# A two-layer hybrid decoder trunk on one core: z gates and output weights moved into the recurrence of layer 1

## The chip, the cores and the metric

The kernel runs on one core of one Trainium2 chip. The metric is the device time of one execution in microseconds (us). Engines are named as in the profile: PE (TensorE matmuls), PEld (its weight loads), DVE (VectorE), ACT (ScalarE), POOL (GpSimd), SP (SyncE, which issues the DMAs). Every engine works through its own instructions in order.

## What is computed

The reference is a trunk of two residual layers over 2048 tokens of width 1024, in float32, with a top-2 mixture of experts behind each mixer. Layer 0 mixes by causal pooling and a convolution. Layer 1, the place of the change, is a gated DeltaNet with 8 heads of width 128:

```python
u = h @ w_in
qkv = silu(causal_depthwise_conv(u[..., :3 * DN_WIDTH], conv_w))
q, k, v = split(qkv)
z = u[..., 3 * DN_WIDTH:4 * DN_WIDTH]
...
v_new = u_i - einsum('bhck,bhkv->bhcv', w_i, state)
o_i = einsum('bhck,bhkv->bhcv', qg_i, state) + einsum('bhcm,bhmv->bhcv', a_i, v_new)
state = state * d_i[..., None, None] + einsum('bhck,bhcv->bhkv', kd_i, v_new)
...
o = o * rsqrt(mean(o * o, -1) + EPS) * onorm_g * silu(z)
y = o @ w_out
x = x + g_m * y
```

The gate silu(z) is not needed before the output projection; q, k and v are needed by the recurrence over chunks, which needs, for each chunk, the inverse of a lower triangular matrix.

## The kernel before

`layer0` and `moe(0)` take the first 1243 us. Layer 1 follows: `mixer1` (`dn_project`, then `dn_chain`), `out_phase(1)`, `moe(1)` and `final`. A tile scheduler orders each engine's instructions when the kernel is built, by priorities that follow the order of the code, and adds the waits; after that the order is fixed.

`dn_project` works on two halves of 1024 tokens, and in each on 8 heads (`dn_head`). A head has four *strips*: 128 output columns of k, q, v and z, in the order k, q, v, z. A strip's 1024x128 weights are loaded by one DMA, split on ACT (`wh`) and DVE (`wl`) into a high and a low part (L237, L238), and multiplied in `proj` as 3 products for each of 8 blocks of the contraction and 2 token halves: 48 matmuls (L260 to L262). k, q and v go through `ub` to a four-tap convolution on DVE (`dacc`, L1218 and L1220) and a Silu on ACT; z gets only a Silu (L1210) and is stored to `zT`. Then PE transposes k and q by blocks (`tk<-ident,kq`, L1230), ACT and DVE take sums of squares (`ssk`, `ssq`), DVE makes `kd`, PE multiplies k by k and q (`tp<-kqh`, L1287), DVE applies the decay (`na`, L1288) and makes `kg` (L1293) and `vp` (L1305). `na`, `kd`, `kg` and `vp` are stored to `stg`. Head by head the scheduler weaves strips of one head into the rest of the other. `egb`, which `kg` reads, has the buffer of `ub`, and `vp` that of `dacc`.

`dn_invert` inverts the diagonal blocks of four heads at a time in 31 steps j of a multiplication and a reduction on DVE (L1321, L1322), whose width grows as j times j. There are four inversions. `pump` lets a head advance one by a number of steps: eight a head. The inversion of half 0's heads 0 to 3 runs in half 0, that of its heads 4 to 7 in heads 0 to 3 of half 1, that of half 1's heads 0 to 3 in the last heads, and the fourth in the recurrence.

`dn_chain` runs 16 blocks of 128 tokens (blocks 0 to 7 read half 0, 8 to 15 half 1). For each block and each group `hg` of four heads, `M` builds the inverse `tt` from the diagonal blocks two blocks ahead, and `R` makes `dv` (L1463: `stin` less a product with the state S), `vt` (by `tt`), the output `po` and the new state S (L1481). `tail` and `O` normalize and transpose the output, and `store` writes it to `yT`. The loads `stin` are issued two blocks ahead into six buffers, in two pools.

`out_phase(1)` begins when the recurrence is over: it loads the eight blocks of `w_out` (L509), splits them (`woh`, `wol`), makes rows of the gate `gm` and the gain on all partitions (`row_bcast`, L199), loads y and z for the first tiles (`yr`, `zr`), multiplies them (L490), and runs `project` for 16 tiles of 128 tokens (`po<-woh,yh`, L536), each followed by the multiplication by `gm` (L540), the residual sum and the norm.

Of the kernel before, what the change touches and what calls it, by code (L numbers as in the profile page):

```python
# [6 lines left out]
F32 = mybir.dt.float32  # L7
# [9 lines left out]
P = 128  # L17
S = 2048
# [23 lines left out]
NYS = 3  # L42

# [27 lines left out]
class Trunk:  # L71
# [120 lines left out]
    def row_bcast(self, psum, src, out):  # L192

        nc = self.nc
        for h in range(2):
            p = psum.tile([P, 512], F32, name="tp")
# [68 lines left out]
    def layer0(self, yT):  # L265
        tc, nc, ins = self.tc, self.nc, self.ins
        with ExitStack() as ctx:
            cv = ctx.enter_context(tc.tile_pool(name="cv0", bufs=1))
            psl = ctx.enter_context(tc.tile_pool(name="psl0", bufs=1, space=PSUM))
# [194 lines left out]
    def out_phase(self, l, yT, xsrc, gm=None, raw=None, cv=None):  # L464
# [4 lines left out]
        with ExitStack() as ctx:  # L469
            ep = lambda name, bufs, **k: ctx.enter_context(tc.tile_pool(name=name, bufs=bufs, **k))  # L470
            wa = ep("woa", 1)
            ys = [ep("yo0", 1), None]
            wb = ep("wob", 1)
            wp = ep("wo", 1)
# [24 lines left out]
            wh = wa.tile([P, KD, D], F32R, name="woh")  # L499
            wl = [p.tile([P, KD // 2, D], F32R, name="wol") for p in (wa, wb)]  # L500
            if raw:
                stage = [raw.tile([P, D], F32, name="wr") for _ in range(KD)]
            else:
# [4 lines left out]
            for k in range(KD):  # L508
                nc.sync.dma_start(stage[k], ins[f"w_out{l}"][k])  # L509
            yin = [load_y(t) for t in range(2)]  # L510
            yin[0] = split_y(0, yin[0])
            for k in range(KD):
                self.prep = self.split(wh[:, k], wl[k // 4][:, k % 4], stage[k])
            if gm is None:
                gm = wp.tile([P, D], F32, name="gm")
                self.row_bcast(pt, self.mod[:, l * 48 + 16:l * 48 + 24], gm)
            ga = wp.tile([P, D], F32, name="ga")
            self.row_bcast(pt, self.gain[l, 1], ga)
            sh = wp.tile([P, D], F32, name="sh")
            self.row_bcast(pt, self.mod[:, l * 48 + 24:l * 48 + 32], sh)  # L520
            wr = wp.tile([P, KD, 36], F32, name="wr")
            nc.sync.dma_start(wr, ins["w_r"][l])
# [5 lines left out]
            def project(t):  # L528
# [11 lines left out]
                nc.vector.tensor_mul(h, ps, gm)  # L540
# [181 lines left out]
    def route_setup(self, pool):  # L722
# [16 lines left out]
        for l in range(2):  # L739
# [8 lines left out]
            self.lists.append(lst)  # L748


    def moe(self, l, raw=None):

# [425 lines left out]
    def pump(self, n):  # L1178
# [3 lines left out]
        with self.tc.issue_after(self.loaded.ins):  # L1182
            next(self.rest, None)
# [513 lines left out]
```

## Time and profile before

| | us |
|---|---|
| median of 3 runs | 3320.69 (3320.61 to 3329.27) |
| the profiled execution | 3314.58 |
| its span, first to last instruction | 3312.9 |
| busy in the span: PE / DVE / ACT / POOL | 2905.9 / 2440.1 / 1495.6 / 1023.9 |
| mean granted clock of PE | 0.943 of full speed |

The profile shows one execution. "Busy" is time in which an engine ran an instruction; the clock is the mean over the stretch of what PE was granted, and 1.00 stands for 2.4 GHz, 0.50 for 1.2 GHz. A row of windows gives the stretch and its length in us, the busy us of each engine with its instructions in brackets, then the clock of PE, the mean busy share of the 16 DMA engines, and GB/s. A timeline row gives when an instruction began; rows of like instructions are drawn together with their count (x14). In brackets stands how long the engine had been idle and which instruction ended that. A matmul's time includes its passage through the array, so neighbouring matmuls overlap: the spacing of their starts is what they cost.

### The profile page before, as it was taken

The page shows a single profiled execution, that of the slowest core. Times are in us where ns is not written, and L with a number is a line of the kernel's source. Part 1 is how long each engine was busy: PE and PEld are TensorE (multiplying, and loading weights), DVE is VectorE, ACT ScalarE, POOL GpSimd, SP SyncE. Part 2 cuts the span into 40 slices and gives each one's busy share as a digit, 9 for nine tenths or more (in the row PEclk, how much of TensorE's full clock was granted, in tenths as well). Part 3 has the DMA queues.
Part 4 walks back from the last instruction along what each step waited for, and adds up shares of the span by engine and source line. Part 5 has one row for each costly group of instructions (what it writes and reads, how often), then busy time and mean ns, then how long its engine had stood idle before and what let it go on. Part 6 is the DMA issues. An engine that isn't in the chain of part 4 may idle for free. (4 is left out here: it accounts for less than half of the span.)

```text
span 3312.9 us, 41950 instructions
## 1 busy us (share of the span) xinstructions
PE 2905.9 (88%) x14192; PEld 2311.3 (70%) x14192; DVE 2440.1 (74%) x3805; ACT 1495.6 (45%) x2560; POOL 1023.9 (31%) x877
## 2 busy tenths in 40 slices
PE   4979878787999997999989999987988996999991
PEld 3756656566777774888867877767986765777770
DVE  4998999757878775767876776858445556888783
ACT  6135233216656546443444433344762224666552
POOL 1142323333444431313212131235530213444431
PEclk9989989888999997999999999998999997999995
DMA  6226233638999854545452343457857437989876
GB/s 222 88 70 213 80 132 127 216 121 302 314 277 302 269 166 156 174 149 192 141 169 87 104 142 114 138 155 220 268 189 223 158 121 251 312 279 298 262 230 217
DMA packets 384987, 633.40 MB, mean 191 GB/s; under 512 B 111232, under 2 KB 245504, under 8 KB 384768
## 3 DMA queue, kind: packets, MB, share of 16 engines
q1 hardware_dynamic: 355904, 563.38, 50.0%
q0 software_dynamic: 28864, 67.30, 8.7%
q8 instruction: 114, 1.87, 0.2%
q14 instruction: 105, 0.86, 0.1%
HBM read 484.46 MB, written 175.44 MB: 199 GB/s over the span
## 5 line engine op out<-in xcount | busy, mean ns | idle before, releaser
L260 PE MATMUL pm<-hh,wh 128*128 128x512 f32 x1408 | 564.9, 402 | 0.8 <-ACT wh L237 0.7
L262 PE MATMUL pm<-hh,wl 128*128 128x512 f32 x1408 | 555.2, 395 | 3.6 <-DVE wl L238 3.6
L261 PE MATMUL pm<-hl,wh 128*128 128x512 f32 x1408 | 554.0, 394 | 4.5 <-DVE hl L233 4.5
L238 DVE TENSOR_TENSOR wl<-wr,wh 128x1024 fp32r<-128x1024 f32 x384 | 452.0, 1217 | 41.6 <-ACT wh L237 38.4
L237 ACT ACTIVATE wh<-wr 128x1024 fp32r<-128x1024 f32 x384 | 399.4, 1057 | 126.4 <-PE pu L819 57.2
L838 POOL DMA_INDIRECT acc<-ys,ixs x102 | 262.8, 2577 | 434.7 <-DVE wl L238 122.0
L261 PEld LDWEIGHTS pm<-hl,wh 128*128 128x128 f32 x1408 | 268.2, 190 | 63.9 <-DVE hl L233 4.9
L260 PEld LDWEIGHTS pm<-hh,wh 128*128 128x128 f32 x1408 | 268.3, 191 | 62.3 <-issue 4.5
L262 PEld LDWEIGHTS pm<-hh,wl 128*128 128x128 f32 x1408 | 267.7, 190 | 62.5 <-DVE wl L238 5.7
L817 PE MATMUL pu<-wh,xt 128*128 128x512 f32 x656 | 268.3, 409 | 0.5 <-ACT xt L237 0.5
L818 PE MATMUL pu<-wl,xt 128*128 128x512 f32 x656 | 260.9, 398 | 0.0
L819 PE MATMUL pu<-wh,xt 128*128 128x512 f32 x656 | 259.8, 396 | 0.0
L238 DVE TENSOR_TENSOR wl<-wraw,wh 128x1024 fp32r<-128x1024 f32 x88 | 110.9, 1260 | 152.1 <-ACT wh L237 152.0
L286 DVE SCALAR_TENSOR_TENSOR acc<-cin,wfir,acc 128x512 f32<-128x512 f32 (+1 forms) x320 | 214.7, 726 | 0.1
L536 PE MATMUL po<-woh,yh 128*128 128x512 f32 x512 | 172.7, 414 | 30.6 <-issue 10.7
L237 ACT ACTIVATE wh<-wraw 128x1024 fp32r<-128x1024 f32 x88 | 93.2, 1059 | 224.5 <-PE pm L261 224.3
L1220 DVE SCALAR_TENSOR_TENSOR dacc<-ub,cols,dacc 128x1024 f32<-128x1024 f32 x144 | 186.7, 1297 | 2.8
L536 PE MATMUL po<-wol,yh 128*128 128x512 f32 x512 | 166.7, 406 | 0.0
L536 PE MATMUL po<-woh,yl 128*128 128x512 f32 x512 | 165.6, 403 | 0.2 <-DVE yl L238 0.2
L795 POOL DMA_INDIRECT xg<-hn,ixs x102 | 112.8, 1106 | 162.5 <-PE tp L805 77.0
L189 POOL TENSOR_TENSOR rs<-rs1t,expo 128x1 f32<-128x1 f32 x48 | 28.3, 589 | 381.3 <-DVE rs1t L187 341.1
L819 PEld LDWEIGHTS pu<-wh,xt 128*128 128x128 f32 x656 | 123.8, 189 | 30.8 <-DVE xt L238 0.5
(377 smaller groups left out, 6359.9 us busy)
## 6 DMA issues: line engine op xcount, KB each, us to landing
wr<-in_w_up_dram SPq DMA_DIRECT2D x256, 512.0 KB, 7.8
wr<-in_w_down_dram SPq DMA_DIRECT2D x128, 512.0 KB, 7.2
modw<-in_modwT_dram SPq DMA_DIRECT2D x96, 512.0 KB, 5.2
wraw<-in_w_in_dram SPq DMA_DIRECT2D x88, 512.0 KB, 3.6
stin<-stg SPq DMA_DIRECT2D x32, 1280.0 KB, 10.5
yr<-yT SPq DMA_DIRECT2D x32, 512.0 KB, 4.2
acc<-xo SPq DMA_DIRECT2D x32, 512.0 KB, 4.1
hn<-ho SPq DMA_DIRECT2D x32, 512.0 KB, 3.1
```

The source lines that it names most:

```text
L237: a = nc.scalar.activation(h, x, AF.Copy) if eng == "act" else nc.vector.tensor_copy(h, x)
L238: return a, nc.vector.tensor_sub(l, x, h.bitcast(F32))
L260: nc.tensor.matmul(ps, wh[:, k], hh[:, k], start=k == 0, stop=False)
L261: nc.tensor.matmul(ps, wh[:, k], hl[:, k], start=False, stop=False)
L262: nc.tensor.matmul(ps, wl[:, k], hh[:, k], start=False, stop=k == KD - 1)
L286: self.tap = nc.vector.scalar_tensor_tensor(o, x, w, i, op0=ALU.mult, op1=ALU.add)
L536: nc.tensor.matmul(ps[:, ns], a[:, k], b[:, ns], start=k == 0 and i == 0, stop=k == KD - 1 and i == 2)
L817: nc.tensor.matmul(ps, xh[:, k], uh, start=k == 0, stop=False)
L818: nc.tensor.matmul(ps, xh[:, k], ul, start=False, stop=False)
L819: nc.tensor.matmul(ps, xl[:, k], uh, start=False, stop=k == KD - 1)
L838: st = nc.gpsimd.indirect_dma_start(out=self.acc, out_offset=bass.IndirectOffsetOnAxis(ap=ix[:, 0:1], axis=0), in_=ys, in_offset=None, bou ...
L1220: nc.vector.scalar_tensor_tensor(acc, ub[:, i:i + 1024], self.col("dn_conv", si * 4 + i), acc, op0=ALU.mult, op1=ALU.add)
```

## The change

In half 1 the z strips leave `dn_head`. `z_strips`, a generator, holds all eight and is handed to `dn_chain`, which runs one strip at each `run(side)` in its first blocks; the weights, the activations hT and z buffers live in pools on the right side of the memory until then. The heads of half 1 advance an inversion by four steps a head (`pump(2 - half)`) instead of eight, so only the second inversion runs there; the third and the fourth run in `dn_chain`, two steps at each `run(invs, invs)`.

When the strips are through, `right.close()` frees their memory and `weights()` follows: it loads the eight blocks of `w_out`, three buffers in turn, multiplies each by the row of the gate (so `out_phase(1)` no longer does), splits it, and makes the rows `ga`, `sh` and `wr` (`out_rows`). `out_phase(1)` finds them in `self.outw`. In `dn_chain`, `dv` is written over `stin`'s VP, `vt` over KE, the decayed state into the next S; `stin` has four buffers (NST) in one pool, `nd`, `ld` and `ot` have fewer, PSUM gives two tiles to the strips and one to `po`. The z tile is half as wide, with two buffers and two stores a strip. All pools take `reuse_waits="tile"`: a tile waits for the tiles whose place it takes.

```diff
-        with ExitStack() as ctx:
-            ep = lambda name, bufs, **k: ctx.enter_context(tc.tile_pool(name=name, bufs=bufs, **k))
+            ep = lambda name, bufs, **k: ctx.enter_context(tc.tile_pool(name=name, bufs=bufs, reuse_waits="tile", **k))
...
+            rp = lambda name, bufs: right.enter_context(tc.tile_pool(name=name, bufs=bufs, side="right", reuse_waits="tile"))
+            wp = rp("w1", 2)
+            hp = rp("h1", 2)
+            self.zs = rp("z1", 1)
...
+                    if half == 0 and hd % 4 == 3:
                         assert next(self.inv, None) is None
-                        self.inv = self.dn_invert(half, hd // 4, wk) if (half, hd) != (1, 7) else iter(())
+                        self.inv = self.dn_invert(half, hd // 4, wk)
+        def z_strips(psum):
+            for hd in range(8):
+                w = self.load_strip(wp, ins["w_in1"][24 + hd], "d")
+                self.z_strip(1, hd, w, hT, psum)
+                yield
+    def z_strip(self, half, hd, w, hT, psum):
+        nc = self.nc
+        for c2 in range(2):
+            zs = self.zs.tile([P, 512], F32, name="zs", bufs=2)
+            ps = psum.tile([P, 512], F32, name="pm")
+            self.proj(ps, w, hT[c2])
+            nc.scalar.activation(zs, ps, AF.Silu)
+            nc.sync.dma_start(self.zT[half][hd, :, c2 * 512:(c2 + 1) * 512], zs)
...
-        self.pump(2)
+        self.pump(2 - half)
-        strip(3)
+        if half == 0:
+            strip(3)
...
+            def weights():
...
+                for k in range(KD):
+                    w = stage[k]
+                    nc.vector.tensor_mul(w, w, gm)
+                    fetch(k + 2)
+                    yield
+                    self.split(wh[:, k], wl[:, k], w)
+                    yield
+                self.outw = (wh, (wl[:, :4], wl[:, 4:]), *self.out_rows(1, wo, pm, "mm"))
...
+            side = chained(zg, close(), weights())
+            invs = chained(self.dn_invert(1, 0, iv), self.dn_invert(1, 1, iv))
+            for bl in range(NT):
...
+                run(t)
+                run(*r)
+                run(invs, invs)
+                run(*m)
+                if bl + 3 < NT:
+                    load_n(bl + 3)
+                if bl > 1:
+                    store(bl - 2)
+                run(side)
+                run(r[0], m[0])
+                run(invs, invs)
+                run(r[1], m[1])
+                run(invs, invs)
+                run(t)
+                run(r[0], m[0])
+                load(*((bl + 2, 0) if NST > 3 else (bl + 1, 1)))
+                run(side)
+                run(invs, invs)
+                run(r[1], m[1])
...
-                nc.vector.tensor_mul(h, ps, gm)
-                nc.vector.tensor_add(x, h, x)
+                if l == 0:
+                    nc.vector.tensor_mul(h, ps, gm)
+                    nc.vector.tensor_add(x, h, x)
+                else:
+                    nc.vector.tensor_add(x, ps, x)
```

Three places show how the order moves. The first is DVE in the burst of a late half-1 head, before. Here `xtmp` and `xblk` are an inversion's step 25, and the `wl` is that of the next head's k strip:

```order
L1288 TENSOR_TENSOR na<-tp,dt 128x512 x2
L238 TENSOR_TENSOR kql<-kq,kqh 128x512 x2
L1293 TENSOR_TENSOR kg<-kq,egb 128x1024
L1288 TENSOR_TENSOR na<-tp,dt 128x512 x2
L1305 TENSOR_TENSOR vp<-tk,nk 128x1024
L1321 TENSOR_TENSOR xtmp<-xblk 128x25x25
L238 TENSOR_TENSOR wl<-wraw,wh 128x1024
L1322 TENSOR_REDUCE xblk<-xtmp 128x25
```

The same place of the change; the `wl` is now that of the next head's q strip:

```order
L1322 TENSOR_TENSOR kg<-kq,egb 128x1024
L1317 TENSOR_TENSOR na<-tp,dt 128x512
L1322 TENSOR_TENSOR kg<-kq,egb 128x1024
L1334 TENSOR_TENSOR vp<-tk,nk 128x1024
L1350 TENSOR_TENSOR xtmp<-xblk 128x25x25
L1351 TENSOR_REDUCE xblk<-xtmp 128x25
L1350 TENSOR_TENSOR xtmp<-xblk 128x26x26
L239 TENSOR_TENSOR wl<-wraw,wh 128x1024
L1351 TENSOR_REDUCE xblk<-xtmp 128x26
```

The `wl` of the k strip has moved ahead of the burst, where z's was, and that of the q strip stands behind `vp` and one and a half steps. In earlier heads of half 1, with narrower steps, it stands behind three.

The second is DVE in block 1 of the recurrence, from the add of the first group's S to behind that of the second, before:

```order
L1481 TENSOR_TENSOR S_18534<-sd_18436,pr 128x512
L1417 STREAM_TRANSPOSE xt_18449<-xh 128x128
L1417 STREAM_TRANSPOSE xt_18457<-xh 128x128
L1481 TENSOR_TENSOR S_18570<-sd_18445,pr 128x512
L1517 TENSOR_SCALAR ot<-mm,cols 128x512
L1447 COPY w_18118<-mm 128x2x64
L1447 COPY w_18120<-mm 128x2x64
L1517 TENSOR_SCALAR ot<-mm,cols 128x512
```

And the change, in which that `wl` belongs to a z strip and the steps to the third inversion:

```order
L1512 TENSOR_TENSOR S_18055<-S_18055,pr 128x512
L1351 TENSOR_REDUCE xblk<-xtmp 128x28
L1350 TENSOR_TENSOR xtmp<-xblk 128x29x29
L1351 TENSOR_REDUCE xblk<-xtmp 128x29
L1350 TENSOR_TENSOR xtmp<-xblk 128x30x30
L1351 TENSOR_REDUCE xblk<-xtmp 128x30
L1350 TENSOR_TENSOR xtmp<-xblk 128x31x31
L1351 TENSOR_REDUCE xblk<-xtmp 128x31
L239 TENSOR_TENSOR wl<-wraw,wh 128x1024
L1512 TENSOR_TENSOR S_18063<-S_18063,pr 128x512
L1546 TENSOR_SCALAR ot<-mm,cols 128x512
L1481 COPY w_17554<-mm 128x2x64
```

Three and a half inversion steps and a `wl` now stand between the two adds, and the copies of `w` behind them.

The third is PE where the recurrence ends and `out_phase(1)` begins, before:

```order
L1514 MATMUL mm<-ident,on_21191 128x128 x4
L1514 MATMUL mm<-ident,on_21196 128x128 x4
L1514 MATMUL mm<-ident,on_21260 128x128 x4
L1514 MATMUL mm<-ident,on_21265 128x128 x4
L199 MATMUL tp<-ident,mod 128x128 x8
L199 MATMUL tp<-ident,gain_13392 128x128 x8
L199 MATMUL tp<-ident,mod 128x128 x8
L536 MATMUL po<-woh,yh 128x512 x2
L536 MATMUL po<-wol,yh 128x512 x2
L536 MATMUL po<-woh,yl 128x512 x2
```

And the change; `ob` has the part of `on`:

```order
L1543 MATMUL mm<-ident,ob_21111 128x128 x2
L1543 MATMUL mm<-ident,ob_21208 128x128 x4
L1543 MATMUL mm<-ident,ob_21227 128x128 x4
L532 MATMUL po<-woh,yh 128x512 x2
L532 MATMUL po<-wol,yh 128x512 x2
L532 MATMUL po<-woh,yl 128x512 x2
L532 MATMUL po<-woh,yh 128x512 x2
```

The transposes for the rows (L199) are gone from here, and the first product of the output phase follows the last transposes of the recurrence.

## Rows read from the trace of the kernel before

**Rows 1.** Windows: us; busy PE, PEld, DVE, ACT, POOL; clock; DMA share; GB/s.

```profile
1780.00:2190.00 410.00, 387.30 (x1852) 321.68 (x1851) 310.31 (x379) 164.11 (x251) 98.46 (x101) 0.99 0.37 117
...
2206.00:2470.00 264.00, 232.84 (x1848) 221.41 (x1848) 150.75 (x369) 157.77 (x592) 132.80 (x128) 0.95 0.74 231
2470.00:2518.00 48.00, 33.44 (x131) 26.03 (x132) 25.72 (x26) 18.27 (x28) 2.19 (x2) 0.72 0.88 275
```

**Rows 2.** Window from the first to the eighth T0 of half 1.

```profile
1794.64:2176.27 381.63, 358.93 (x1714) 297.80 (x1713) 290.54 (x355) 150.33 (x224) 91.51 (x90) 0.99 0.38 121
```

**Rows 3.** Timeline of PE in half 1: start, duration, line, instruction.

```profile
1794.64 1.91 PE L1230 MATMUL tk<-ident,kq 128*128 128x128 f32 x16
...
2117.22 1.91 PE L1230 MATMUL tk<-ident,kq 128*128 128x128 f32 x16
...
2176.04 0.39 PE L262 MATMUL pm<-hh,wl 128*128 128x512 f32 x1
2176.27 1.36 PE L1230 MATMUL tk<-ident,kq 128*128 128x128 f32 x11
```

**Rows 4.** Groups by line, half-1 heads: busy us, mean ns; idle before, releaser.

```profile
L1321 DVE TENSOR_TENSOR xtmp<-xblk 128x49 f32<-128x49 f32 (+30 forms) x56 | 50.1, 895 | 1.4 <-POOL xblk L1315 0.2
L238 DVE TENSOR_TENSOR wl<-wraw,wh 128x1024 fp32r<-128x1024 f32 x29 | 35.4, 1221 | 66.9 <-ACT wh L237 66.9
...
L1322 DVE TENSOR_REDUCE xblk<-xtmp 128x7 f32<-128x49 f32 (+30 forms) x56 | 30.2, 539 | 1.2
...
L1266 ACT ACTIVATE dt<-dt,brr 128x128 f32<-128x128 f32 x64 | 19.5, 387 | 1.1 <-DVE brr L1262 1.1
```

**Rows 5.** Timeline of DVE, head that begins at 2117.22.

```profile
2119.42 0.75 DVE L1218 TENSOR_SCALAR dacc<-ub,cols 128x1024 f32<-128x1024 f32 x1
...
2124.92 1.28 DVE L1220 SCALAR_TENSOR_TENSOR dacc<-ub,cols,dacc 128x1024 f32<-128x1024 f32 x1
...
2136.89 1.21 DVE L1305 TENSOR_TENSOR vp<-tk,nk 128x1024 f32<-128x1024 f32 x1
...
2139.23 1.22 DVE L238 TENSOR_TENSOR wl<-wraw,wh 128x1024 fp32r<-128x1024 f32 x1
```

**Rows 6.** Timeline of PE: two waits, in brackets idle time and releaser.

```profile
2001.51 0.44 PE L1230 MATMUL tk<-ident,kq 128*128 128x128 f32 x2 [3.34 <-ACT kq L1225]
...
2591.43 1.94 PE L564 MATMUL tp<-ident,ho 128*128 128x128 f32 x8 [4.75 <-DVE ho L547]
```

**Rows 7.** Windows of the 6 us behind those two waits.

```profile
2001.50:2007.50 6.00, 5.94 (x26) 4.78 (x27) 5.21 (x7) 1.15 (x3) 0.30 (x2) 1.00 0.21 78
2591.40:2597.40 6.00, 5.97 (x18) 3.55 (x19) 4.07 (x5) 2.35 (x4) 0.53 (x1) 0.50 0.96 284
```

**Rows 8.** Window from the eighth T0 to block 5 of the recurrence.

```profile
2176.27:2313.42 137.15, 107.54 (x712) 96.23 (x710) 99.45 (x193) 64.70 (x221) 72.35 (x71) 0.88 0.71 218
```

**Rows 9.** Timeline of DVE, last inversion step in the recurrence.

```profile
2306.75 2.48 DVE L1321 TENSOR_TENSOR xtmp<-xblk 128x961 f32<-128x961 f32 x1
...
2309.34 1.15 DVE L1322 TENSOR_REDUCE xblk<-xtmp 128x31 f32<-128x961 f32 x1
```

**Rows 10.** Waits of PE in that stretch: us in total, times, longest.

```profile
PE pr L1379 <- DVE dv L1463: 7.0, 5, 3.4
PE mm L1438 <- DVE tl L1434: 4.6, 8, 0.8
```

**Rows 11.** Window of one later block of the recurrence.

```profile
2374.00:2388.65 14.65, 13.97 (x122) 13.71 (x122) 7.15 (x20) 10.10 (x38) 8.97 (x10) 1.00 0.88 268
```

**Rows 12.** Timeline of PE between recurrence and output phase.

```profile
2472.42 2.53 PE L1514 MATMUL mm<-ident,on 128*128 128x128 f32 x8 [5.12 <-ACT on L1507]
...
2493.10 1.19 PE L536 MATMUL po<-woh,yh 128*128 128x512 f32 x2 [10.67 <-issue]
```

**Rows 13.** Timeline of DVE between those two.

```profile
2484.04 5.77 DVE L238 TENSOR_TENSOR wol<-wr,woh 128x1024 fp32r<-128x1024 f32 x5 [2.01 <-ACT woh L237]
```

**Rows 14.** Groups by line, output phase of layer 1, DVE.

```profile
L540 DVE TENSOR_TENSOR ho<-po,gm 128x1024 f32<-128x1024 f32 x15 | 18.3, 1222 | 45.6 <-PE po L536 45.6
```

More of the change, by code (lines that the diff above doesn't have):

```diff
@@ L42 @@
 NYS = 3
+NST = 4
 def slots():
@@ L497, in split_y @@
                 return yh, yl
[L499 to L503, printed above, removed]
+            if l == 0:
+                wh = wa.tile([P, KD, D], F32R, name="woh")
+                wl = [p.tile([P, KD // 2, D], F32R, name="wol") for p in (wa, wb)]
                 both = wk.tile([P, 2, D], F32, name="wraw", tag="hT", bufs=1)
@@ new lines, in dn_chain, with behind @@
+            both = lambda bl: [load(bl, hg) for hg in range(2)]
+            with tc.high_priority(offset=400):
+                load_n(0)
+                both(0)
+                load_n(1)
+                load(1, 0)
+                if NST > 3:
+                    load(1, 1)
+                last = load_n(2)
+            na, kg, vp = self.stores[-3:]
+            def behind(st, ld):
+                tc.add_manual_dep(st.ins, ld.ins.name,
+                                  mybir.DependencyInfo(mybir.DependencyClass.NoSync, mybir.DependencyReason.DATA),
+                                  reason="issued after the first loads")
@@ new lines, in dn_chain, with chained, close @@
+            behind(na, last)
+            zg = zgen(pz)
+            run(zg)
+            for sd in (kg, vp):
+                behind(sd, last)
+            g = [M(0, 0), M(0, 1)]
+            nxt = [M(1, 0), M(1, 1)]
+            run(*g)
+            for i in range(5):
+                run(*g)
+                if i == 1:
+                    run(*nxt)
+            def chained(*gens):
+                for g in gens:
+                    yield from g
+            def close():
+                right.close()
+                yield
@@ new lines, in dn_chain @@
+            side = chained(zg, close(), weights())
+            invs = chained(self.dn_invert(1, 0, iv), self.dn_invert(1, 1, iv))
+            for bl in range(NT):
+                r = [R(bl, 0), R(bl, 1)]
+                m, nxt = nxt, [M(bl + 2, hg) if bl < NT - 2 else iter(()) for hg in range(2)]
+                t = tail(bl - 1) if bl else iter(())
+                oss[bl] = self.small.tile([P, 2, 4], F32, name="oss")
+                run(t)
[17 more added lines that the diff above has]
+                run(r[1], m[1])
+                load(*((bl + 2, 1) if NST > 3 else (bl + 2, 0)))
+                run(invs, invs)
+                if bl:
+                    O(bl - 1, 0)
+                run(*m)
+                run(invs, invs)
+                if bl:
+                    O(bl - 1, 1)
+                run(*nxt)
+                run(*m)
+                if bl == 4:
+                    for _ in invs:
+                        pass
@@ L1604, in pack @@
+            for _ in side:
+                pass
+            for _ in tail(NT - 1):
+                pass
+            for hg in range(2):
+                O(NT - 1, hg)
+                if hg == 0:
+                    store(NT - 2)
+            store(NT - 1)
 def pack(inputs):
```

266 lines of the change are left out of this document (104 added, 162 removed).

## The prediction

> **What bounds the kernel now.** I read the stages first [rows 1]. They all belong to layer 1, which is where the change moves instructions. In the half-1 heads PE is busy for 387.3 of 410 us at a clock of 0.99: that stage is bound by PE. In the recurrence (2206 to 2470) it is 232.8 of 264, and in the 48 us after it 33.4 at a clock of 0.72. So what can be won without taking work away from PE lies in the recurrence and behind it.
>
> The heads are told by the time between the transposes `tk<-ident,kq` of neighbouring heads; I call that moment T0. From the first T0, 1794.64, to the eighth, 2176.27 [rows 3], there are seven periods in 381.6 us, 54.5 us each, with PE busy for 358.9 [rows 2], 51.3 a head. A strip is 48 matmuls a weight block, two token halves by 24, and they follow each other at 0.23 us [rows 3], so 10.9 us. A head has four.
>
> In such a head DVE works through a burst that starts at T0: the last strip's taps, sums of squares, `kd`, `na`, `kg`, `vp`. In the last full head it ran from 2119.42 to 2138.1, with the `wl` of the next strip at 2139.23 [rows 5]. The z strip is what PE does meanwhile.
>
> **The change: the heads.** Every half-1 head loses its z strip, its `wl` and four of its eight inversion steps. If PE stayed full this would be 7 × 10.9 = 76 us plus the 22.7 that PE idles today (381.6 - 358.9), 99 in all. It cannot stay full: the order of DVE puts the `wl` of the next head's q strip behind `vp` and up to three inversion steps, and PE has only the k strip before it. From that head: `vp` ends 20.9 us after T0 (2117.22 [rows 3]). Without the z strip's `wl` (1.2) and one of two inversion steps in it (2.0) it would end at 17.7; I add 2 for `na`, whose factors ACT scales in 3.1 us (eight of 0.39 [rows 4]). Then come one or two inversion steps (the mean step is 0.90 + 0.54 us [rows 4]), and `wl`, 1.2: that is T0 + 23 to 24, and I let the q strip run freely from T0 + 24. Behind that stand two strips, 21.8, with a few transposes. A period is then 45.9 and seven are 321: **-60 us**. Ends: -99 (PE full), and -22 (every period as long as its PE work of today, idle in the place of z). I take the first sum, as its rows are the nearest.
>
> PE now has some 5.5 us of idle in each head, in pieces of up to 3. Rows on what that does to the clock: after an idle of 3.34 us the next 6 us ran at 1.00; after one of 4.75 the next 6 us ran at 0.50, which is 1.2 in place of 2.4 GHz, and 6 us at half speed lose 3 us [rows 6, 7]. I keep the clock at 1.00, for the pieces are nearer to the first.
> The Trainium skill speaks against this part ("TensorE: Matmul & The Clock Gate", HAM oscillation — how this bites in real kernels): a loop that lets TensorE idle once in every pass falls to the cold clock in every pass and pays the return each time. The trace agrees on single gaps; by that rule 21 us of this term would be lost, and the sum below would be -7.
>
> **The first blocks.** From the eighth T0 to block 5's `tt` product at 2313.42 there are 137.15 us, PE busy for 107.5 at a clock of 0.88 [rows 8]. A clock of 0.88 is 24% of the time, 33 us, at half speed; with PE busy for about 26 of them, 13 us come back at full speed, which leaves 94.5. The seven moved strips add 76: 171 is the floor. Waits stay. Right behind T0 no strip is left: PE needs some 3 us for the transposes (eleven in 1.36 [rows 3]) and twelve `kqh` products, then stands for `vT` and for `na`. The last tap ended 9.0 us after T0 [rows 5], 7.8 without the `wl` ahead of it, and the Silu follows: 9 us of waiting in two pieces. In block 1 the order puts four inversion steps and a `wl` between the two adds on S, and the copy of `w` behind both. The last step measures 2.48 + 1.15 us [rows 9]; the four with the `wl` are about 10 us, and PE has some 4 us of other work there: 6 us. In block 2 a like piece: 4 us. That makes 190, **+53 us**. Ends: 171 (+34), and 171 plus the 29.6 that PE idles there today (+63). I stay between: of today's waits on DVE, 7.0 us on `dv` and 4.6 on `tl` [rows 10], the strips cover the first, but not what stands behind the second inversion.
>
> **Blocks 5 to 15.** A block takes 14.65 us with PE at 13.97, DVE at 7.15, ACT at 10.10 and DMA at 0.88 [rows 11]. A weight adds 2.4 us to DVE (1.22 for gm [rows 14], 1.2 for the split [rows 4]), one copy to ACT, and 0.52 MB, which is 36 GB/s on 268: DVE and ACT have room, DMA comes to 1.0. **+1 us**; the ends are -2 (the two long blocks behind the old inversion shorten) and +10 (every load late by an eighth of a block).
>
> **The start of the output phase.** Today the last transposes run at 2472.42 and the first product at 2493.10, after an idle of 10.67 [rows 12], in which DVE splits the weights, five of them in 5.77 us, and loads follow [rows 13]. Weights, rows and gate are now ready, and the order has the product right behind the transposes. I put it at 2477, for PSUM must be handed over: **-16 us** (ends -10 and -20; if `yr` and `zr` were late, the -10).
>
> **The tiles.** The multiplication by gm, 1.222 us a tile [rows 14], goes. PE covers it except where a group of tiles ends and PE waits for `ho`, as at 2591.43 for 4.75 us [rows 6]: 3 or 4 times, **-4 us** (0 to -8). **Leaner waits** in layer 0 and both MoE stages move no row and free a wait here and there; I take **-2** (0 to -6).
>
> Sum: -60 + 53 + 1 - 16 - 4 - 2 = **-28 us** on the profiled execution, 3314.6 (span 3312.9). The median of the runs, 3320.7, is 0.18% above it, so I forecast **3293 us**. Its own range, from the middle of each term's bounds, is 3273 to 3311.
>
> **Rivals.**
> (1) *PE stays nearly full.* If the order hides the burst behind the k strip and `wl` comes at T0 + 21, a head falls to 43 us, -80 in all, and the strips cover the waits of block 1 and 2, +42: the sum is -59, 3262 us. For it: DVE, busy for 290.5 us in seven heads [rows 2], 41.5 in one, loses four steps and a `wl` and falls to some 35 of 43 us. Against it: its order is fixed and `vp` alone ends at about T0 + 20.
> (2) *The clock falls once a head.* If the pieces of idle run together, 3 us are lost at each of 7 heads and 3 waits of the first blocks: +30, the sum is +2, 3323 us, no change. For it: the row at 4.75 us; against it: the one at 3.34.
> (3) *Slower: the clock falls twice a head,* at the wait for `vT` and at the wait for `wl`. Then 6 us are lost in each of 7 heads, 42, and 12 in the first blocks: +54, the sum is +26, 3347 us. It decides from 4 us lost a head (28 / 7). Against it: the k strip of 10.9 us lies between the two waits.
>
> **How the numbers follow.** Chances: the forecast 0.48, rival 1 0.15, rival 2 0.20, rival 3 0.17. About 0.3%, 10 us, is what a measurement of this kernel can tell from no change. Of the forecast 0.45 is faster and 0.03 the same; rival 1 is all faster; of rival 2 0.03 is faster, 0.14 the same and 0.03 slower; of rival 3 0.01 is the same and 0.16 slower. Faster 0.63, same 0.18, slower 0.19. The range 3260 to 3338 leaves out somewhat under half of rival 1 (0.07) and three quarters of rival 3 (0.13), 0.2 in all.
>
> **What would show it.** T0 to T0 near 46 us, with idle of PE put down to `wl`, and a clock of 1.00 in the heads; if it stands below 0.97, rival 2 or 3. From the eighth T0 to block 5 near 190 us, with waits for `w` in block 1. Blocks of 14.65 us from 5 on. The first `po<-woh` within 5 us of the last transposes of the recurrence. The prediction is wrong if the heads stay above 50 us, or if the first blocks take over 202.

## The result, and the profile after

The changed kernel is **slower**: 3359.14 us median of 4 runs (3356.39 to 3366.02) against 3321.01 (3320.61 to 3329.27) in the same session, a ratio of 1.012 [1.0107, 1.0133]. I had forecast 3293 us, and 3260 to 3338 as the range. The profiled execution has a span of 3358.3 us for 3312.9, +45.4 (the medians differ by 38.1); its mean clock is 0.942 for 0.943.

Cut at the same moments as in the prediction, the two spans compare as follows (us; each end is the start of a PE row, T0 is the `tk<-ident,kq` between two heads, "block n" its first `tt` product):

| stage | before | after | difference | forecast |
|---|---|---|---|---|
| up to the first T0 | 1794.6 | 1795.3 | +0.6 | 0 |
| seven half-1 heads | 381.6 | 359.5 | -22.1 | -60 |
| eighth T0 to block 5 | 137.2 | 211.4 | +74.3 | +53 |
| block 5 to block 15 | 147.4 | 169.1 | +21.7 | +1 |
| block 15 to the first `po<-woh` | 32.3 | 15.3 | -17.0 | -16 |
| output phase, to the first transposes of the MoE | 277.5 | 267.0 | -10.5 | -4 |
| MoE and final norm | 542.3 | 540.7 | -1.6 | -2 (with the first row) |

So the start of the output phase and its tiles came as forecast or better, the last small term came to half of what I had put, and the three large ones all came out worse. The windows of those three, after (columns as in [rows 1]); they answer to [rows 2], [rows 8] and, for a block, [rows 11]:

```profile
1795.28:2154.80 359.52, 299.53 (x1375) 241.76 (x1374) 249.35 (x294) 137.94 (x204) 89.95 (x89) 0.91 0.35 110
2154.80:2366.23 211.43, 180.50 (x1052) 159.95 (x1050) 150.27 (x266) 84.56 (x245) 72.26 (x66) 0.92 0.61 184
2366.23:2535.33 169.10, 149.65 (x1214) 140.73 (x1214) 87.62 (x211) 115.68 (x392) 89.67 (x84) 1.00 0.69 215
2502.78:2519.13 16.35, 14.98 (x122) 13.99 (x122) 8.51 (x23) 10.93 (x39) 9.18 (x9) 1.00 0.56 195
```

In the heads PE is now busy for 299.5 of 359.5 us where it was 358.9 of 381.6, at a clock of 0.91 for 0.99. In the first blocks busy time rose by 73.0, about the seven moved strips, idle time stayed (30.9 for 29.6), and 34 us still passed at half speed (a clock of 0.92 is 16% of 211 at half, against 24% of 137). A later block takes 16.35 us for 14.65, at a clock of 1.00, though no weight is prepared in it (the last `wol` starts at 2465.9): PE idles for 1.4 us in it where it was 0.7, and its busy time, in which a matmul's own passage counts, is 15.0 for 14.0.

**The heads.** PE's waits in that stretch, after (us in total, times, longest):

```profile
PE tk L1258 <- ACT kq L1253: 49.7, 7, 7.1
```

There are seven heads and seven waits of 7 us for `kq`: the transposes of k at the end of each head. PE in the head that begins at 2051.34:

```profile
2051.34 1.69 PE L1258 MATMUL tk<-ident,kq 128*128 128x128 f32 x14
...
2071.41 0.50 PE L261 MATMUL pm<-hh,wh 128*128 128x512 f32 x1 [1.06 <-ACT ub L1243]
...
2082.19 0.39 PE L263 MATMUL pm<-hh,wl 128*128 128x512 f32 x1
2089.68 0.69 PE L1258 MATMUL tk<-ident,kq 128*128 128x128 f32 x2 [7.11 <-ACT kq L1253]
...
2102.96 1.69 PE L1258 MATMUL tk<-ident,kq 128*128 128x128 f32 x14
```

The q strip began at T0 + 20.1 and ended at 2082.6; then PE stood for 7.11 us, because the transposes of k come next in its order. Those need the Silu of k, that needs the four taps, and here is DVE in the same head, then ACT, then SP:

```profile
2052.39 1.23 DVE L239 TENSOR_TENSOR wl<-wraw,wh 128x1024 fp32r<-128x1024 f32 x1 [5.88 <-ACT wh L238]
...
2070.59 1.21 DVE L1334 TENSOR_TENSOR vp<-tk,nk 128x1024 f32<-128x1024 f32 x1
...
2075.44 1.21 DVE L239 TENSOR_TENSOR wl<-wraw,wh 128x1024 fp32r<-128x1024 f32 x1
...
2079.03 0.91 DVE L1351 TENSOR_REDUCE xblk<-xtmp 128x27 f32<-128x729 f32 x1
2080.93 0.75 DVE L1246 TENSOR_SCALAR dacc<-ub,cols 128x1024 f32<-128x1024 f32 x1 [0.98 <-DMA stg<-vp]
2083.48 1.23 DVE L239 TENSOR_TENSOR wl<-wraw,wh 128x1024 fp32r<-128x1024 f32 x1 [1.80 <-ACT wh L238]
2084.62 3.92 DVE L1248 SCALAR_TENSOR_TENSOR dacc<-ub,cols,dacc 128x1024 f32<-128x1024 f32 x3
```

```profile
2082.39 1.06 ACT L238 ACTIVATE wh<-wraw 128x1024 fp32r<-128x1024 f32 x1 [9.60 <-PE pm L262]
...
2088.57 1.06 ACT L1253 ACTIVATE kq<-dacc 128x1024 f32<-128x1024 f32 x1 [3.83 <-DVE dacc L1248]
```

```profile
2071.11 4.39 SPq L1328 DMA_DIRECT2D ndia<-na  x4
2075.54 0.94 SPq L1330 DMA_DIRECT2D noff<-na  x2
2076.58 0.40 SPq L1227 DMA_DIRECT2D stg<-vp  x1
```

Read backwards: `kq` at 2088.57 waits for the last three taps, which start at 2084.62. Between them and the first tap DVE has a `wl`, that of the k strip behind v, whose `wh` waited 9.60 us on ACT, for the q strip's last use of that weight buffer. The first tap, at 2080.93, waited for the DMA `stg<-vp`: `dacc` lies in the buffer of `vp`. `vp` itself ended at 2071.8; its store was issued 4.8 us later, behind four `ndia` and two `noff` DMAs in SP's queue, and took another 4.2 us. Three inversion steps fill DVE meanwhile, so that its idle time shows only the last 0.98 us of it. Over the seven heads DVE waits for this store in six (us in total, times, longest):

```profile
DVE dacc L1246 <- DMA stg<-vp: 18.4, 6, 5.5
```

These rows also show that I had named a `wl` wrongly. The text on the change and the prediction take the `wl` behind `vp` for that of the q strip. Counted one by one, every strip has one `wl`, in the order of the strips: the one at 2052.39 is that of q, and the one behind `vp`, at 2075.44, is that of v. The q strip had begun at 2071.41, 4 us before the `wl` that was to hold it. In the rows of before it is the same: the `wl` at 2139.23 [rows 5] is that of q, not of k, whose products run from 2138.06 at the latest.

In the kernel before, the chain was the same in the head of [rows 5]. DVE, then SP, in that head:

```profile
2154.82 0.76 DVE L1218 TENSOR_SCALAR dacc<-ub,cols 128x1024 f32<-128x1024 f32 x1
```

```profile
2137.41 4.56 SPq L1299 DMA_DIRECT2D ndia<-na  x4
2142.02 0.94 SPq L1301 DMA_DIRECT2D noff<-na  x2
2143.06 0.40 SPq L1193 DMA_DIRECT2D stg<-vp  x1
```

`vp` had ended at 2138.1 [rows 5], its store was issued 5.0 us later, and the first tap of the next k came at 2154.82, with no wait: the z strip stood ahead of the k strip on PE, and by the last product of k, at 2148.5, the store had landed. PE waited 3.39 us for `kq` in this head and 7.11 us after the change. The z strip was the cover of this chain (run 1 tries it).

Part of the chain did get longer. In four of the seven heads before, the store of `vp` was issued ahead of the six small DMAs, and in none of these did PE wait for `kq`; in the other three it stood behind them, as it does in all seven after, and PE waited. No run tried that order by itself.

The wait also costs clock. Windows of that head: up to the wait, the wait, the 6 us behind it, and the rest:

```profile
2051.34:2082.30 30.96, 28.90 (x147) 23.47 (x145) 28.11 (x32) 12.47 (x20) 12.84 (x10) 1.00 0.51 159
2082.30:2089.68 7.38, 0.28 (x2) 0.00 (x0) 4.99 (x4) 3.44 (x4) 0.19 (x1) 0.83 0.23 71
2089.68:2095.70 6.02, 6.01 (x19) 4.70 (x20) 4.61 (x4) 1.16 (x3) 0.33 (x2) 0.65 0.00 0
2095.70:2102.96 7.26, 7.26 (x33) 5.96 (x32) 1.29 (x2) 2.61 (x5) 0.05 (x1) 1.00 0.00 0
```

**The end of the recurrence.** After, the first product of the output phase, which answers to [rows 12]:

```profile
2547.28 2.53 PE L1543 MATMUL mm<-ident,ob 128*128 128x128 f32 x8 [5.18 <-ACT ob L1537]
2550.65 1.22 PE L532 MATMUL po<-woh,yh 128*128 128x512 f32 x2 [0.84 <-DVE ot L1546]
```

It begins 3.4 us after the last transposes do, where there were 20.7 us.

### The profile page after: what moved, and what is told of

The parts are those of the page before. It is cut to its first block, busy times and chain, and to the rows that moved or that the text cites. A ratio compares the mean times of both kernels' runs of the same rounds, so it can differ in the third digit from the quotient of the medians.

```text
span 3358.3 us, 41933 instructions
## 1 busy us (share of the span) xinstructions
PE 2918.4 (87%) x14192; PEld 2313.9 (69%) x14192; DVE 2439.9 (73%) x3797; ACT 1505.3 (45%) x2558; POOL 1032.9 (31%) x877
## 5 line engine op out<-in xcount | busy, mean ns | idle before, releaser
L261 PE MATMUL pm<-hh,wh 128*128 128x512 f32 x1408 | 571.7, 407 | 4.5 <-ACT ub L1243 3.6
L532 PE MATMUL po<-woh,yh 128*128 128x512 f32 x512 | 172.8, 414 | 20.3 <-ACT yh L238 10.9
L828 PEld LDWEIGHTS pu<-wh,xt 128*128 128x128 f32 x656 | 123.8, 189 | 30.7 <-DVE xt L239 0.4
L826 PEld LDWEIGHTS pu<-wh,xt 128*128 128x128 f32 x656 | 124.1, 189 | 29.0 <-ACT xt L238 1.5
```

Of the source, the lines that this page charges most:

```text
L261: nc.tensor.matmul(ps, wh[:, k], hh[:, k], start=k == 0, stop=False)
L532: nc.tensor.matmul(ps[:, ns], a[:, k], b[:, ns], start=k == 0 and i == 0, stop=k == KD - 1 and i == 2)
L826: nc.tensor.matmul(ps, xh[:, k], uh, start=k == 0, stop=False)
L828: nc.tensor.matmul(ps, xl[:, k], uh, start=False, stop=k == KD - 1)
```

## The experiments

My first theory (A in most runs): the half-1 heads are set by the chain above and not by PE, so the z strip was nearly free there and costs its full PE time in the recurrence. The rivals: PE's order holds a ready v strip behind k's transposes; or the inversions that were moved along are the loss. The stages of all runs, in us (columns as in the table above, without the first row), and the ratio to the kernel before, timed beside it. The row left out, up to the first T0, lies between 1792.5 and 1799.5 us in these profiles, though no edit aims at it, so a few us between two spans tell nothing:

| kernel | heads | first blocks | 5 to 15 | to `po` | tiles | MoE | span | median | ratio |
|---|---|---|---|---|---|---|---|---|---|
| before | 381.6 | 137.2 | 147.4 | 32.3 | 277.5 | 542.3 | 3312.9 | 3321.0 | 1 |
| after | 359.5 | 211.4 | 169.1 | 15.3 | 267.0 | 540.7 | 3358.3 | 3359.1 | 1.012 [1.0107, 1.0133] |
| 1 z in the heads | 366.7 | 137.6 | 198.4 | 15.3 | 265.5 | 542.0 | 3322.2 | 3325.0 | 1.0003 [0.9992, 1.0015] |
| 2 tail later | 359.7 | 206.5 | 160.3 | 17.2 | 266.7 | 542.1 | 3348.2 | 3349.8 | 1.0078 [1.0048, 1.0107] |
| 3 k transposes behind v | 360.9 | 210.0 | 171.9 | 15.3 | 266.1 | 543.0 | 3359.6 | 3363.1 | 1.0118 [1.0088, 1.0147] |
| 4 weights last | 359.4 | 210.3 | 159.1 | 33.5 | 265.9 | 542.5 | 3363.9 | 3366.3 | 1.0127 [1.0098, 1.0157] |
| 5 weights only | 383.3 | 142.8 | 164.3 | 14.7 | 265.1 | 541.1 | 3305.7 | 3309.0 | 0.9969 [0.9957, 0.9982] |
| 6 wl behind taps | 334.4 | 209.7 | 172.0 | 15.3 | 267.4 | 541.7 | 3333.9 | 3335.7 | 1.0046 [1.003, 1.0062] |
| 7 no chain | 301.2 | 210.5 | 168.4 | 15.3 | 267.5 | 541.2 | 3300.3 | 3300.7 | 0.994 [0.992, 0.996] |
| 8 tail later, osq 2 | 359.4 | 206.6 | 156.1 | 14.7 | 267.2 | 542.9 | 3346.4 | 3344.4 | 1.0071 [1.0049, 1.0094] |
| 9 = 7 and 8 | 301.2 | 203.8 | 156.2 | 14.7 | 265.9 | 541.7 | 3280.7 | 3283.2 | 0.9884 [0.9867, 0.99] |
| 10 = 9, third inversion in heads | 311.1 | 199.7 | 153.4 | 16.5 | 266.6 | 541.8 | 3282.6 | 3285.5 | 0.9894 [0.9876, 0.9912] |
| 11 wl and vp | 293.0 | 211.8 | 168.5 | 15.3 | 267.3 | 540.7 | 3290.1 | 3296.3 | 0.9922 [0.9896, 0.9949] |
| 12 = 11 and 8 | 293.0 | 208.4 | 156.3 | 14.7 | 264.9 | 540.9 | 3275.1 | 3277.3 | 0.9861 [0.9845, 0.9877] |

**1. The z strips back in the heads.** All else as after.

```diff
-        if half == 0:
-            strip(3)
+        strip(3)
...
-                w = self.load_strip(wp, ins["w_in1"][24 + hd], "d")
-                self.z_strip(1, hd, w, hT, psum)
                 yield
```

> Undoes one part: the z strips of half 1 go back into their heads, nothing else of the change is undone. Theory A (the heads lost their cover to a wait of 7.1 us each, and the moved strips lengthen the first blocks by about what they cost): T0 to T0 rises from 51.4 to about 52, seven periods from 359.5 to about 364 us; from the eighth T0 to block 5 the time falls from 211 to 140 to 150 us; the whole falls by 55 to 65 us against the change, to about 3300 us. Theory B (not the strips but the two inversions in the recurrence make its first blocks long): that stretch stays above 170 us, and the whole falls by less than 40 us.

The first blocks fell by 73.8 us to 137.6, the length of before; the heads rose by 7.2. So seven strips cost 7 us in the heads and 74 in the first blocks. The other 15 us that the heads gained after (381.6 to 366.7) are the four inversion steps a head that left: run 5 has them back, at 383.3. The stages are those of theory A, but the whole fell by 36.1 us in the span, which is not A's 55 to 65 and within B's 40: blocks 5 to 15 got 29.3 longer, most of it a single wait, for the fourth inversion, which the shorter first blocks no longer cover. So the two stages show a loss of 67 by the move, and the whole keeps 36 of it, the main part of the 45 us. PE at block 8:

```profile
2377.66 1.89 PE L1456 MATMUL mm<-xt,na 128*128 128x32 f32 x8 [25.77 <-DVE xt L1448]
```

**2. The output's factors and scaling later.** ACT's `ob<-ob,fac` waits for a factor that comes over POOL and DVE, and stands in front of `tt`, for which PE waits. The waits in blocks 5 to 15, after:

```profile
ACT ob L1537 <- DVE fac L1533: 23.7, 11, 2.9
...
PE mm L1485 <- ACT tt L1486: 6.9, 6, 1.3
```

The edit puts both behind `dv` and `vt` of the two groups:

```diff
-                run(t)
+                with tc.issue_after(self.vt.ins), (tc.issue_after(self.dv.ins) if bl else ExitStack()):
+                    run(t)
```

> Undoes one part: the second step of tail, in which ACT scales the output of the block before by fac, is held back again behind vt and the subtraction from VP, as before the change. Theory A (in blocks 5 to 15 ACT stands 2.9 us for fac in front of the copy to tt, and PE stands behind that): a block falls from 16.4 to about 15 us, blocks 5 to 15 from 170 to about 154 us, the whole by 12 to 18 us. Theory B (the single buffers of po and osq, or the output weights, lengthen the blocks): the blocks shorten by less than 0.5 us each and the whole by less than 5 us.

Blocks 5 to 15 lost 8.8 us, the first blocks 4.9, and the wait for `fac` is gone. That is a part, and short of the 154 us of theory A; blocks of 16.0 us are left.

**3. The transposes of k behind the v strip on PE.**

```diff
-        pk = tok(lambda b: kq[:, b, 0])
+        with (self.tc.issue_after(self.lastmm.ins) if half else ExitStack()):
+            pk = tok(lambda b: kq[:, b, 0])
```

> Changes one order: in half 1 the transposes of k are held back until the last matmul of the head's v strip, so that two of them no longer stand ahead of that strip on PE. Theory A (the 7.1 us before them is a wait that PE's order puts in front of a strip that is ready): the wait goes, T0 to T0 falls from 51.4 to 44 to 46 us, the clock in the heads rises from 0.91 to 1.00, and the whole falls by 40 to 50 us. Theory B (the chain of DVE and ACT from ub over the taps to the Silu sets the head's length, whatever PE's order): the wait appears again before the transposes at T0, a head stays above 50 us and the whole falls by less than 10 us.

A miss for PE's order as the cause: the heads take 360.9 us, and the wait only has another name. PE's first wait in the heads of this run:

```profile
PE pm L261 <- ACT ub L1243: 55.4, 10, 7.6
```

The v strip needs the `pm` that q still holds, `ub` is one buffer, and k's taps read it. The chain holds both ways.

**4. The output weights prepared behind block 15** and not beside the blocks.

```diff
-            side = chained(zg, close(), weights())
+            side = chained(zg)
+            late = chained(close(), weights())
...
+            for _ in late:
+                pass
```

> Moves one part: the output weights and rows are made when the recurrence is over instead of beside its blocks 4 to 12. Theory A (they cost the blocks little and save their whole time at the start of the output phase): blocks 5 to 15 shorten by 2 to 6 us, the stretch from the last block to the first output product grows from 15 to 35 to 45 us, and the whole rises by 15 to 25 us. Theory B (their DVE, ACT and DMA work is what lengthens the blocks): blocks 5 to 15 fall by 15 us or more and the whole stays within 10 us.

Blocks 5 to 15 lost 10.0 us, between the two theories, and the start of the output phase took 18.2 more (the longest of three waits of PE there is below). Preparing the weights in the recurrence costs 10 and brings 18: more than half of what it brings is paid back where I had put +1. Whether DVE, ACT or DMA makes the 10 is not shown.

```profile
2547.50 1.36 PE L1543 MATMUL mm<-ident,ob 128*128 128x128 f32 x4 [15.08 <-ACT ob L1537]
```

**5. What is left of the change without the moved strips and the moved third inversion:** z in the heads, eight inversion steps a head, only the fourth inversion in the recurrence, and the edits of run 8.

```diff
-            invs = chained(self.dn_invert(1, 0, iv), self.dn_invert(1, 1, iv))
+            invs = chained(self.dn_invert(1, 1, iv))
...
-        self.pump(2 - half)
+        self.pump(2)
```

> The kernel after, with the z strips back in the half-1 heads, eight inversion steps a head and only the fourth inversion in the recurrence as before, the factors and scaling of a block's output ordered behind dv and vt of both groups, and two osq buffers. What stays of the change: weights, rows and gate prepared in the recurrence, the leaner buffers, tile-wise waits. Theory A (the moved strips and the moved third inversion are the whole loss, and the prepared weights gain what their stage showed): seven heads 375 to 382 us, eighth T0 to block 5 137 to 142, blocks 5 to 15 152 to 160, the first product of the output phase 15 to 18 us behind block 15, its tiles 266: span 3283 to 3296, ratio to before 0.990 to 0.995. Theory B (what the weights gain in the output phase they take in the recurrence, by DVE, ACT or DMA): blocks 5 to 15 165 or more, span 3305 to 3316, no change from before.

Between the two theories, and nearer to B: faster than before by 0.3%, where A had 0.5 to 1.0%; the span lies in B's range, and blocks 5 to 15, at 164.3, end 0.7 short of it. The heads are those of before, and the output phase gains. The longest wait of PE in its recurrence, below, ends at 2206.0, in the first blocks, where the kernel before has one of 7.0 us for the same tile; it is 3 of the 5.6 us by which that stage is longer than before. Why blocks 5 to 15 take 8.2 us more than in run 8, which has the same edits to them, stays open. PE's waits in its recurrence, the first row:

```profile
PE mm L1456 <- POOL na L1385: 10.7, 2, 10.2
```

**6. The `wl` that waits for its buffer behind the taps on DVE.** `self.taps` holds the last tap of each strip.

```diff
-        self.split(wh, wl, w)
+        nc.scalar.activation(wh, w, AF.Copy)
+        with (self.tc.issue_after(behind.ins) if behind else ExitStack()):
+            nc.vector.tensor_sub(wl, w, wh.bitcast(F32))
...
+            w = self.load_strip(wp, ins["w_in1"][which * 8 + hd], "d", behind=self.taps[-3] if half else None)
```

> The kernel after, with the DVE half of a strip's weight split (wl) ordered behind the taps of the strip three earlier, in half 1; nothing else. Theory A (in each head a wl that waits for its weight buffer stands on DVE ahead of the k strip's taps and holds kq, PE's next work, by about 2.9 us): seven heads 335 to 345 us (359.5 in the kernel after), span 3333 to 3345. Theory B (the store of vp, whose buffer the taps wait for, sets the head alone, and the wl only fills its time): heads 355 to 360, span 3352 to 3360.

334.4 us, 0.6 below the range of A: the place of one instruction a head on DVE is worth 25.1 us. The wait of PE for `kq` fell from 49.7 us to 28.0, and in six of the seven heads the store alone holds the first tap now. PE's waits and DVE in one head of this run:

```profile
PE tk L1261 <- ACT kq L1256: 28.0, 7, 7.1
```

```profile
2045.78 1.21 DVE L1337 TENSOR_TENSOR vp<-tk,nk 128x1024 f32<-128x1024 f32 x1
...
2056.31 0.75 DVE L1248 TENSOR_SCALAR dacc<-ub,cols 128x1024 f32<-128x1024 f32 x1 [1.20 <-DMA stg<-vp]
2057.10 3.92 DVE L1250 SCALAR_TENSOR_TENSOR dacc<-ub,cols,dacc 128x1024 f32<-128x1024 f32 x3
```

**7. The whole chain cut:** run 6, `vp` in a buffer of its own (paid for by two instead of three buffers of `modw`), and the second inversion at eight steps in heads 0 to 3, none in heads 4 to 7.

```diff
-            self.rest = self.mod_rest(cv, [(1, i) for i in range(16, 48)], tag="modw", bufs=3)
+            self.rest = self.mod_rest(cv, [(1, i) for i in range(16, 48)], tag="modw", bufs=2)
...
-        vp = self.last.tile([P, 8, P], F32, name="vp", tag="dacc", bufs=1)
+        vp = self.last.tile([P, 8, P], F32, name="vp", bufs=1)
...
-        self.pump(2 - half)
+        self.pump(2)
```

> The kernel after, with three edits to the half-1 heads: wl ordered as in the run before, vp in a buffer of its own (the prefetch of the modulation weights gets two buffers for three to pay for it), and the second inversion at eight steps a head in heads 0 to 3 and none in heads 4 to 7. Theory A (the chain vp, its store, taps, ub sets the head, not PE): heads 4 to 7 have periods of 43 to 46 us, heads 0 to 3 46 to 49, seven heads 315 to 332, clock in the heads above 0.95. Theory B (each wait removed is followed by the next in the same place, because DVE, ACT and the single buffers of ub, kq, dt are all in the chain): seven heads 345 to 358. The first blocks should not move by either (211 us).

Better than A: 301.2 us, and the last three periods take 40.9 us each. The first blocks stayed at 210.5, as expected.

**8. Run 2 with two buffers of `osq`.**

```diff
-                    sq = wk.tile([P, P], BF16, name="osq", bufs=1)
+                    sq = wk.tile([P, P], BF16, name="osq", bufs=2)
```

> The kernel after, with the factors and scaling of a block's output ordered behind dv and vt of both groups, as in the run that did that alone (blocks 5 to 15 160.3 us), and two buffers for osq instead of one. Theory A (ACT's queue sets a block, and eight Square pairs at .43 instead of .31 us are a part of it): blocks 5 to 15 149 to 153 us, span 3336 to 3342. Theory B (the one PSUM buffer of po, whose copy waits on ACT, sets it): 157 to 161, span 3346 to 3350.

156.1 us for blocks 5 to 15, 4.2 below run 2, and below the range of B but above that of A; the span, 3346.4, lies in that of B. With one buffer a Square starts 0.44 us behind the one before, with two 0.29; the first row pair below is of after, the second of this run:

```profile
2509.35 0.31 ACT L1520 ACTIVATE osq<-ob 128x128 bf16<-128x128 f32 x1
...
2509.79 0.31 ACT L1520 ACTIVATE osq<-ob 128x128 bf16<-128x128 f32 x1
```

```profile
2469.89 0.29 ACT L1520 ACTIVATE osq<-ob 128x128 bf16<-128x128 f32 x1
...
2470.18 0.29 ACT L1520 ACTIVATE osq<-ob 128x128 bf16<-128x128 f32 x1
```

PE still waits for the one `po` nine times, 5.3 us in all. The 8.7 us that remain against before are about what run 4 puts on the weights (10.0).

**9 and 10. All gaining edits; then the third inversion back in heads 4 to 7.** The second differs by `invs = chained(self.dn_invert(1, 1, iv))` and by a third `dn_invert` in the heads, as before.

> The kernel after with the edits that gained, together: wl ordered behind the taps, vp in its own buffer, the second inversion at eight steps a head in heads 0 to 3 of half 1, the factors and scaling behind dv and vt of both groups, two osq buffers. Theory A (the heads' chain and ACT's order in the blocks are separate losses): the parts add up, seven heads 301 us, eighth T0 to block 5 203 to 208, blocks 5 to 15 154 to 158, span 3281 to 3290, ratio to before 0.987 to 0.992. Theory B (what is won early is waited for later, at a load or a store): blocks 5 to 15 above 163, span 3295 or more.

> The kernel of the run beside it (all gaining edits), with the third inversion at eight steps a head in heads 4 to 7 of half 1, as before, so that only the fourth is left in the recurrence. Theory A (in the first blocks PE's idle time, 30.9 us in the kernel after, is mostly DVE working on inversion steps ahead of x2t, tl and ot): the first blocks fall by 12 to 17 us to 189 to 195, the heads rise by 10 to 15 to 311 to 316, and the span stays within 5 us of the run beside it. Theory B (the inversions only fill time there; the strips and the half clock set the first blocks): they fall by less than 5, the heads rise by the same 10 to 15, and the span is 5 to 12 us longer than that of the run beside it.

The parts add up: 9 is faster than before, by 1.2%. In 10 the first blocks fell by only 4.1 us, the heads rose by 9.9, the span by 1.9. B holds for the stage, and A for the span. PE's longest waits in the first blocks, run 9, then run 10:

```profile
PE mm L1483 <- DVE x2t L1477: 7.1, 1, 7.1
PE tk L1261 <- ACT vT L1254: 6.8, 1, 6.8
...
PE mm L1475 <- DVE tl L1471: 4.4, 3, 3.5
```

```profile
PE tk L1261 <- ACT vT L1254: 8.2, 1, 8.2
...
PE mm L1475 <- DVE tl L1471: 1.2, 3, 0.5
```

The 7.1 us for `x2t` were inversion steps; they are gone, and `tl` fell from 4.4 to 1.2. The wait for `vT` behind the eighth T0 stays in all runs with the strips moved (6.8 to 8.2 us).

**11. Run 7 with the inversion left at four steps a head.**

> The kernel after with wl ordered behind the taps and vp in its own buffer, but the second inversion at four steps a head in all eight half-1 heads, as in the kernel after. Theory A (the buffer that vp shares with the taps was the larger part of the head's chain): seven heads 298 to 312 us. Theory B (it was the inversion steps, which fill DVE in the same place): 325 to 334, as with wl alone (334.4).

293.0 us, below A's range: the shared buffer of `vp` was worth 41.4 us on top of run 6 (a run with that buffer alone is missing), and bunching the steps in run 7 had cost 8.2. The windows of the heads and PE's waits of this run:

```profile
1793.59:2086.60 293.01, 281.26 (x1379) 231.10 (x1378) 245.97 (x294) 136.46 (x204) 97.29 (x89) 1.00 0.43 134
```

```profile
PE tk L1261 <- ACT kq L1256: 1.4, 1, 1.4
```

The clock is 1.00, and PE is busy for 281.3 us with the work that took 299.5 after: 18.3 us of the loss lie in busy time, most of it half clock (in the head shown above, 6.02 us at 0.65 are 4.2 at half speed, 2.1 lost), and 48.2 in idle time (60.0 less 11.8). DVE in a head of this run, where the first tap starts 3.9 us after `vp` does and not 10.3:

```profile
1933.96 1.22 DVE L1337 TENSOR_TENSOR vp<-tk,nk 128x1024 f32<-128x1024 f32 x1
...
1937.88 0.75 DVE L1248 TENSOR_SCALAR dacc<-ub,cols 128x1024 f32<-128x1024 f32 x1
```

**12. Runs 11 and 8 together**, the fastest version found.

> The kernel after with wl ordered behind the taps, vp in its own buffer, the factors and scaling behind dv and vt of both groups and two osq buffers, and the second inversion left at four steps a head. By the parts: seven heads 293 us (run of wl and vp), eighth T0 to block 5 204 to 207, blocks 5 to 15 156, the rest as measured: span 3270 to 3278, ratio to before 0.985 to 0.988. If the heads give back what they win at the first loads of the recurrence, the first blocks come to 212 or more and the span to 3280.

3277.32 us, 1.4% faster than before and, by the medians, 2.4% faster than after. Only the first blocks came out above the parts, by 1.4 us.

## Why the prediction was wrong, step by step

**The heads, forecast -60, measured -22.1: the step that failed is "I let the q strip run freely from T0 + 24".** The q strip did start early, at T0 + 20.1: the `wl` behind `vp`, which I had made its gate, is that of the v strip. And its end was not the end of the waiting: my period has nothing between the q strip and the v strip, and there PE stood for 7.1 us in each head, 49.7 in seven. The gate was behind that `wl`: the next head's taps, which wait for `vp`'s store through a shared buffer, and a `wl` that waits for a weight buffer in front of the taps. I named the shared buffer of `dacc` and `vp` in the description of the kernel and put no price on it. Runs 6 and 11 price the two, one on top of the other: 25.1 and 41.4 us, 66.5 together, and with both gone the heads fall by 88.6, further than my rival 1 (-80). What the removal of work could bring was thus right at the far end of my bounds; the order as built gave three quarters of it away.

**The clock.** I kept it at 1.00; it was 0.91. The wait was more than twice as long as the pieces of up to 3 us that I had, and the row that I went by was one of three. The heads of the kernel before have three such waits, of 3.16, 3.34 and 3.39 us; I had taken the middle one, with 1.00 behind it, and behind the other two the 6 us ran at 0.72. PE's waits for `kq` in those heads of the kernel before, then the windows behind the first and the third:

```profile
PE tk L1230 <- ACT kq L1225: 9.9, 3, 3.4
```

```profile
1944.28:1950.28 6.00, 6.00 (x22) 4.89 (x23) 4.91 (x5) 1.86 (x3) 0.19 (x1) 0.72 0.09 15
2163.17:2169.17 6.00, 6.00 (x22) 4.93 (x23) 4.91 (x5) 1.86 (x3) 0.19 (x1) 0.72 0.00 0
```

Rival 2, one fall in each head, is what happened, at 18.3 us in seven heads, 2.6 each where I had priced 3; but it came on top of the longer idle time. The Trainium skill's rule that I weighed there ("TensorE: Matmul & The Clock Gate", HAM oscillation — how this bites in real kernels) would have had this fall in every pass of the loop; this trace agrees, with one fall at each of the seven waits, in the head shown 0.65 in the 6 us behind the wait and 1.00 after them. Rival 3, the slower side, had two falls a head and no more idle time: the sign was right, the mechanism was not.

**The first blocks, forecast +53, measured +74.3, outside the bounds (+34 to +63).** The strips themselves were sized well: PE's busy time rose by 73.0, and run 1 takes 73.8 off. Two terms beside them failed. "13 us come back at full speed" did not come: 34 us at half clock, as before (33), and I had subtracted those 13 from both bounds. And idle time stayed at 30.9 where I had 19: strips fill PE between waits, but the waits behind the eighth T0 (`vT` 7.0 us) and behind the inversions (`x2t` 7.2) are new or longer. Run 10 shows that the third inversion is worth only 4.1 us of the stage. Why the clock did not recover was not tried on its own.

**Blocks 5 to 15, forecast +1, measured +21.7.** "DVE and ACT have room" was read from busy shares, and those are as low as I had them (ACT 10.9 of 16.35 us). What counted was the order in ACT's queue, `fac` in front of `tt`, 8.8 us (run 2); the one `osq` buffer, 4.2 (run 8); and the weights beside the blocks, 10.0 (run 4). These sum to 23.0 for the 21.7 measured, though no run takes out all three. DMA did not come to 1.0; its share was 0.69. The leaner buffers, to which I gave no price at all, are in the second.

**The rest came near.** The start of the output phase -17.0 (forecast -16), and run 4 shows that the prepared weights make it. The tiles -10.5, better than the end of -8, without a run that tells why. The leaner waits -1.6, with +0.6 ahead of the first T0, so -1.0 for -2, less than the runs scatter.

Against the sum, the errors are +38 in the heads, +21 in the first blocks and +21 in the blocks; -7 in the tiles is all that stood against them.

## What to carry to other kernels

Before work is taken out of a loop because the engine there is full, follow the longest chain of the loop without it: through the DMA that must land before a shared buffer is written again, the queue in which that DMA stands, and any instruction that waits in front of the next link. Here the strip that looked like load was the cover, and 74 us of PE time were moved into a stage whose own idle time, 31 us, they left as it was; with two edits, one buffer and one place in an order, the kernel with the move is 0.8% faster than before (run 11). No run has these edits with the strips left in the heads, so what the move by itself then brings is not shown. An engine that is two thirds busy has no room if the instruction that others wait for stands behind one that itself waits.

## What the runs showed of the hardware that I had not expected

Issuing six small DMAs took longer than a large one took to land: the four `ndia` and two `noff` DMAs, 32 KB each, held SP for 5.3 us (4.39 and 0.94) ahead of the 512 KB store of `vp`, which landed 4.2 us after its own issue. And the clock answers to the pieces in which PE idles: with one wait of 7.1 us a head the heads ran at 0.91 on average, and with no wait of PE longer than 1.4 us in them (run 11) at 1.00; behind the waits of 3.16 to 3.39 us of the kernel before it was 0.72 twice and 1.00 once.
